# Two narrow projections with high and low weights side by side, and operands moved to multiples of 512 bytes

## The chip, the cores and the metric

The kernel runs on one core of a Trainium2 chip. The metric is the time of one execution on the device in microseconds (us), as the median of several runs. The engines are TensorE (PE; its weight loads are PEld), VectorE (DVE), ScalarE (ACT), GpSimd (POOL) and SyncE (SP), which here only issues loads. Each works through a queue of its own in order, and they wait for each other by semaphores.

## The reference, cut to what matters

A trunk of two layers over 256 tokens of width 2048, all in 32-bit floats. Layer 0 mixes with stick-breaking attention and gated linear attention, layer 1 with a Mamba-2 state-space mixer. Each layer ends in a squared-ReLU MLP and a gated embedding per layer.

```python
for i in range(2):
    hn = rms_norm(h, norm_mix[i])
    h = h + (sb_gla_mixer(hn, ...) if i == 0 else ssd_mixer(hn, ...))
    h = h + square(relu(rms_norm(h, norm_mlp[i]) @ w_up)) @ w_down
    h = h + sigmoid(h @ ple_w_gate[i]) * (p[i] @ ple_w_proj[i])
return rms_norm(h, final_norm)
```

Each mixer begins with one wide product of `hn` whose columns are then split. Two of the pieces are narrow. In layer 0 it is the gate rank: `glr`, 16 columns wide, goes through `sigmoid` and sums into the decays of the linear attention. In layer 1 it is `dt`, 64 columns: `dt = softplus(hn @ w + dt_bias)`, and the running sum of `dt * a` over each chunk of 128 tokens gives the decays of all 64 heads.

## The kernel before

**The products.** Every long product is made from reduced-precision pieces. A weight is split into a high part `whi` (a cast on ScalarE, L90) and the rest `wlo` (a subtract on VectorE, L91), and so is `x`; an `x` page holds for one slice of 128 features the 256 high values of all tokens and then the 256 low ones, 512 columns. In `feature_major` (L119 to L145) 128 weight columns are stationary and `x` moves: `whi` against all 512 columns (L130) gives hi·hi in the left half of a bank of PSUM and hi·lo in the right half, `wlo` against the 256 high columns (L135) adds lo·hi to the right half. `add_halves` (L167 to L173) puts the two together: ScalarE copies the right half out (L170), VectorE adds it to the left (L171) and in mixer 1 multiplies by the norm's factor (L173). `token_major` (L159 to L161) and the down product of the MLP (L344 to L346) have the weights as the moving operand of 512 columns, three products for a piece.

**The blocks.** Weights come in blocks of 128 x 2048 floats (1 MB, `load_block`, L102) through three buffers `wraw` on SyncE's queue. Each block is split in two halves of 1024 into three pairs of buffers `whi` and `wlo`. The MLP has a second set of such buffers in a pool of its own, and uses both in turn. A group of 512 weight columns takes four blocks, which is eight halves of 8 + 8 products.

**The narrow projections.** `ab_glr` (mixer 0) and `ssd_dt` (mixer 1, where the first x group follows) use `feature_major` with `width=1, kts=16`: the 16 or 64 columns are padded on the host to 128, so each is one block of 1 MB, two casts, two splits, 16 products of 512 columns and 16 of 256.

**After ssd_dt.** `dt_steps` computes softplus as a series on VectorE, some twenty small instructions on 64 x 256 values (L610 to L626; L614 is a reciprocal, L620 the series, L626 the running sum), which interleave with the convolution (L648), the gating (L179) and the scaling of `x` by the gain (L112, its input `hn` from GpSimd). The running sum goes out to memory (`acs_rows`, L627) and comes back broadcast over all partitions (`rb`, L659), both issued from ScalarE's queue; TensorE transposes `dt` and the sums (L631, L632). The first user of `rb` is L675 on VectorE (tile `mt`).

**What sets the order.** The code is a set of Python generators that are advanced in turn; the framework's scheduler then fixes the order of each engine's queue when the kernel is built. So an edit can move instructions far from its own line.

**Addresses.** Tiles are placed one behind the other in each pool. The profile and the built order show no addresses; from the tile sizes, the pages of `x` and the buffers of the pool `wts` (wraw, whi, wlo) begin at multiples of 512 bytes. The pool of the MLP (its whi, wlo and wsum) and four constants of mixer 0 begin 64 bytes past one, `h` 128 bytes and `ident` 384.

## Time and profile before

| | |
|---|---|
| runs | 2745.70, 2743.98, 2745.56 us; median 2745.56 |
| the profiled execution | 2747.21 us, of which its span on the core 2745.5 |
| granted clock of TensorE, mean | 0.996 |
| TensorE busy | 2711.9 us (14036 products); weight loads 2282.7 |
| VectorE, ScalarE, GpSimd busy | 1914.1, 1421.1, 167.5 us |
| loads | 511.69 MB, 186 GB/s on average |

In a timeline, a row gives the start and the busy time of one or several like instructions in us, then engine, line, operation, output and inputs with shapes and count; a bracket is idle time of the engine ahead of it and what ended it. Successive instructions overlap at their ends, so that the time from one start to the next is the price of an instruction, a little under its busy time. A line number is that of the kernel before; the same code stands 2 lines lower in the changed kernel up to L143, and 27 lines lower from there.

### The profile page before, as it was taken

How to read it: one execution, taken by the hardware profiler on the slowest of the kernel's cores; microseconds unless marked ns; L12 is line 12 of the kernel's file. 1: busy time of each engine (PE TensorE's matmuls, PEld its weight loads, DVE VectorE, ACT ScalarE, POOL GpSimd, SP SyncE). 2: the span in 40 equal slices, each digit the busy share in tenths (PEclk: the TensorE clock that was granted, in tenths of full speed). 3: DMA queues.
4: the chain of work that ended last, by engine and by line, in shares of the span. 5: the costliest groups of instructions: out<-in, count | busy, mean ns of one | idle time of the engine just before them, and what ended most of it. 6: DMA issues, size and time to landing. Idle time of an engine off the chain costs nothing.

```text
span 2745.5 us, 35718 instructions
## 1 busy us (share of the span) xinstructions
PE 2711.9 (99%) x14036; PEld 2282.7 (83%) x14036; DVE 1914.1 (70%) x2569; ACT 1421.1 (52%) x1933; POOL 167.5 (6%) x258
## 2 busy tenths in 40 slices
PE   8999999999999999999999999999999999999998
PEld 6888878888888888888888888888888888888886
DVE  7455666676867767558987878754677776776755
ACT  6455455545545445556555655644454544535544
POOL 2000000000000000002132122300000000000000
PEclk9999999999999999999999999999999999999999
DMA  6544355555555555454555555455555555555543
GB/s 246 186 167 153 123 184 184 199 187 195 201 184 198 186 191 206 176 185 157 197 197 180 192 190 179 170 188 194 184 200 186 209 188 184 186 197 187 214 178 146
DMA packets 73305, 511.69 MB, mean 186 GB/s; under 512 B 8672, under 2 KB 8864, under 8 KB 12464
## 3 DMA queue, kind: packets, MB, share of 16 engines
q1 hardware_dynamic: 70640, 498.63, 50.9%
q10 hardware_dynamic: 2496, 10.78, 1.1%
q8 instruction: 110, 1.80, 0.3%
q14 instruction: 59, 0.48, 0.0%
HBM read 507.21 MB, written 2.16 MB: 186 GB/s over the span
## 4 chain that ended last, share of the span: by engine, by line
PE 96%; DVE 2%; ACT 1%; issue 0%; DMA 0%; POOL 0%; DVEq 0%; ACTq 0%
PE acc L130 31%; PE acc L135 16%; PE q L344 8%; PE q L346 8%; PE q L345 8%; PE acct L160 6%; PE acct L159 6%; PE acct L161 6%; DVE wlo L91 1%; PE y_ps L718 1%; PE x_tp L253 1%; PE y_ps L720 0%; DVE x L112 0%; DVE a_cv L648 0%; ACT whi L90 0%
## 5 line engine op out<-in xcount | busy, mean ns | idle before, releaser
L91 DVE TENSOR_TENSOR wlo<-wraw,whi 128x1024 fp32r<-128x1024 f32 (+1 forms) x940 | 1137.6, 1217 | 657.7 <-ACT whi L90 653.5
L90 ACT CAST whi<-wraw 128x1024 fp32r<-128x1024 f32 x940 | 969.8, 1038 | 1027.4 <-PE acc L130 488.8
L130 PE MATMUL acc<-x,whi 128*128 128x512 f32 x3872 | 1224.0, 399 | 9.9 <-ACT whi L90 9.9
L135 PEld LDWEIGHTS acc<-x,wlo 128*128 128x128 f32 x3872 | 725.0, 189 | 178.4 <-DVE wlo L91 10.0
L135 PE MATMUL acc<-x,wlo 128*128 128x256 f32 x3872 | 761.0, 279 | 7.3 <-DVE wlo L91 7.3
L130 PEld LDWEIGHTS acc<-x,whi 128*128 128x128 f32 x3872 | 596.6, 189 | 19.3 <-ACT whi L90 10.1
L344 PE MATMUL q<-whi,hid 128*128 128x512 f32 x884 | 350.0, 396 | 0.1
L346 PE MATMUL q<-whi,hid 128*128 128x512 f32 x884 | 347.3, 393 | 0.0
L345 PE MATMUL q<-wlo,hid 128*128 128x512 f32 x884 | 344.9, 390 | 0.0
L346 PEld LDWEIGHTS q<-whi,hid 128*128 128x128 f32 x884 | 165.9, 188 | 39.8
L345 PEld LDWEIGHTS q<-wlo,hid 128*128 128x128 f32 x884 | 166.1, 188 | 37.1
L344 PEld LDWEIGHTS q<-whi,hid 128*128 128x128 f32 x884 | 166.0, 188 | 35.4 <-ACT whi L90 0.5
L159 PE MATMUL acct<-whi,x 128*128 128x512 f32 x384 | 151.0, 393 | 0.0
L161 PE MATMUL acct<-whi,x 128*128 128x512 f32 x384 | 149.8, 390 | 0.0
L160 PE MATMUL acct<-wlo,x 128*128 128x512 f32 x384 | 149.7, 390 | 0.0
L90 ACT CAST whi<-wsum 128x1024 fp32r<-128x1024 f32 x56 | 58.9, 1051 | 80.5 <-PE q L346 53.4
L161 PE MATMUL acct<-whi,yx 128*128 128x512 f32 x256 | 100.3, 392 | 0.0
L160 PE MATMUL acct<-wlo,yx 128*128 128x512 f32 x256 | 100.2, 391 | 0.0
L159 PE MATMUL acct<-whi,yx 128*128 128x512 f32 x256 | 100.2, 391 | 0.0
L91 DVE TENSOR_TENSOR wlo<-wsum,whi 128x1024 fp32r<-128x1024 f32 x56 | 68.5, 1223 | 30.1 <-ACT whi L90 30.1
L170 ACT COPY right<-acc 128x256 f32<-128x256 f32 x198 | 72.2, 368 | 27.2 <-PE acc L135 27.1
L161 PEld LDWEIGHTS acct<-whi,x 128*128 128x128 f32 x384 | 72.1, 188 | 15.0
(283 smaller groups left out, 2357.1 us busy)
## 6 DMA issues: line engine op xcount, KB each, us to landing
wraw<-in_mlp_up_dram SPq DMA_DIRECT2D x128, 1024.0 KB, 4.8
wraw<-in_mlp_down_dram SPq DMA_DIRECT2D x128, 1024.0 KB, 4.8
wraw<-in_ssd_in_dram SPq DMA_DIRECT2D x80, 1024.0 KB, 4.8
wraw<-in_ab_in_dram SPq DMA_DIRECT2D x47, 1024.0 KB, 4.8
wraw<-in_ple_gate_dram SPq DMA_DIRECT2D x32, 1024.0 KB, 4.8
wraw<-in_ssd_out_dram SPq DMA_DIRECT2D x32, 1024.0 KB, 4.8
wraw<-in_ab_out_dram SPq DMA_DIRECT2D x16, 1024.0 KB, 4.8
rb<-acs_rows ACTq DMA_DIRECT2D x8, 1024.0 KB, 4.8
```

Of the source, the lines that this page charges most:

```text
L90: nc.scalar.copy(out=hi, in_=src_raw)
L91: nc.vector.tensor_tensor(out=lo, in0=src_raw, in1=hi.bitcast(F32), op=ALU.subtract)
L130: nc.tensor.matmul(banks[n], lhsT=hi[:, o : o + P], rhs=xt(k), start=(k == 0), stop=False, skip_group_check=True)
L135: nc.tensor.matmul(banks[n][:, T : 2 * T], lhsT=lo[:, o : o + P], rhs=xt(k)[:, 0:T], start=False, stop=(k == kb_n * kts - 1), skip_group_c ...
L159: nc.tensor.matmul(banks[n], lhsT=xh, rhs=wh, start=(k == 0), stop=False, skip_group_check=True)
L160: nc.tensor.matmul(banks[n], lhsT=xh, rhs=wl, start=False, stop=False, skip_group_check=True)
L161: nc.tensor.matmul(banks[n], lhsT=xl, rhs=wh, start=False, stop=(k == kb_n * kts - 1), skip_group_check=True)
L170: nc.scalar.copy(out=right[:rows], in_=bank[:rows, T : 2 * T])
L253: nc.tensor.transpose(tp[:, j * T + t * P : j * T + t * P + P], h[:, t, (k + j) * P : (k + j + 1) * P], ident)
L344: nc.tensor.matmul(banks[b], lhsT=ah, rhs=wh, start=b not in begun, stop=False, skip_group_check=True)
L345: nc.tensor.matmul(banks[b], lhsT=ah, rhs=wl, start=False, stop=False, skip_group_check=True)
L346: nc.tensor.matmul(banks[b], lhsT=al, rhs=wh, start=False, stop=end and last[b] == m, skip_group_check=True)
```

## The change

Two things are done. First, spare tiles are put in, and `ident` is moved up, so that the operands of the long products begin at multiples of 512 bytes: what moves are `h`, `ident`, the MLP's second whi and wlo, its wsum, and the constants of mixer 0. The pages and the buffers of `wts` stay on multiples as they were.

Second, `narrow_major` takes the place of `feature_major` for the two narrow projections. The weights come unpadded (32 columns for ab_glr, which has 16; 64 for ssd_dt), a load of 256 KB or 512 KB into a tile of its own. High and low part lie side by side in one tile, so that 64 or 128 stationary columns [high, low] meet the 512 moving columns of `x` in one product: 16 products of 512 in all. The bank then holds hi·hi and hi·lo in its upper rows and lo·hi and lo·lo in its lower ones; `add_parts` copies out and adds the first three.

```diff
-    ev.tile([P, 8], F32, tag="spare", name="spare")
+    ev.tile([P, 136], F32, tag="spare", name="spare", bufs=1)
...
+    keep.tile([P, 96], F32, name="spare0")
     h = keep.tile([P, 2, D], F32, name="h")
+    ident = keep.tile([P, P], F32, name="ident")
...
-    keep.tile([P, 8], F32, name="spare")
+    keep.tile([P, 40], F32, name="spare1")
...
+    def narrow_major(src, cn, xt, evac, pool):
+
+        raw = pool.tile([P, KT, cn], F32, name="nraw")
+        nc.sync.dma_start(raw, src)
+        both = pool.tile([P, KT, 2, cn], F32R, name="wboth")
+        nc.scalar.copy(out=both[:, :, 0, :], in_=raw)
+        nc.vector.tensor_tensor(out=both[:, :, 1, :], in0=raw, in1=both[:, :, 0, :].bitcast(F32), op=ALU.subtract)
+        bank = acc_ps.tile([P, 512], F32, tag="acc", name="accn")
+        for k in range(KT):
+            nc.tensor.matmul(bank[: 2 * cn], lhsT=both[:, k, :, :].rearrange("p a c -> p (a c)"), rhs=xt(k),
+                             start=(k == 0), stop=(k == KT - 1), skip_group_check=True)
+        yield
+        evac(bank)
+        yield
+
+    def add_parts(dst, bank, cn, scale=None):
+        right = ev.tile([P, T], F32, tag="right", name="right")
+        low = ev.tile([P, T], F32, tag="right", name="low")
+        nc.scalar.copy(out=right[:cn], in_=bank[:cn, T : 2 * T])
+        nc.scalar.copy(out=low[:cn], in_=bank[cn : 2 * cn, 0:T])
+        nc.vector.tensor_tensor(out=dst, in0=bank[:cn, 0:T], in1=right[:cn], op=ALU.add)
+        nc.vector.tensor_tensor(out=dst, in0=dst, in1=low[:cn], op=ALU.add)
+        if scale is not None:
+            nc.vector.tensor_tensor(out=dst, in0=dst, in1=scale, op=ALU.mult)
...
-                add_halves(u, bank, 64, rstd[:64])
+                add_parts(u, bank, 64, rstd[:64])
...
-                        yield from feature_major([[ssd_dt]], 1, xu, evac_dt, width=1, kts=16)
+                        yield from narrow_major(ssd_dt, 64, xu, evac_dt, mid)
...
-                add_halves(glr, bank)
+                add_parts(glr[:32], bank, 32)
...
-                yield from feature_major([[ab_glr]], 1, x, evac_glr, width=1, kts=16)
+                yield from narrow_major(ab_glr, 32, x, evac_glr, mid)
```

The load, the cast (L152) and the subtract (L153) of the narrow weights have buffers of their own, so the scheduler puts them where it has room: for ab_glr among the first blocks of mixer 0, for ssd_dt into the first gate of the embedding of layer 0, between two of its loads (SyncE), casts and splits. In mixer 1 some hundred rows of VectorE and fifty of ScalarE around ssd_dt change places; nearly everything else keeps its order. ScalarE's issue of `rb` (L686 there) stood ahead of the cast of the fourth half of the next group, and now stands behind it (the cast of `whi_10892`).

Three places on VectorE's queue follow. The first is the middle of the group after ssd_dt in mixer 1: `dt_work` holds the series, `a_cv` the convolution, `bc0` its gated result, and `wlo_...` are the splits for which TensorE waits. Before:

```order
L613 TENSOR_SCALAR dt_work_10557<-dt_work_10557 64x256
L179 SCALAR_TENSOR_TENSOR bc0_10217<-th_10571,a_cv_10566 128x256
L614 RECIPROCAL dt_work_10557<-dt_work_10557 64x256
L648 SCALAR_TENSOR_TENSOR a_cv_10634<-xp_10484,cw_9986,a_cv_10634 128x256
L615 TENSOR_TENSOR dt_work_10557<-dt_work_10557 64x256
L648 SCALAR_TENSOR_TENSOR a_cv_10634<-xp_10484,cw_9986,a_cv_10634 128x256
L616 TENSOR_TENSOR dt_work_10557<-dt_work_10557 64x256
L91 TENSOR_TENSOR wlo_10653<-wraw_10650,whi_10652 128x1024
L179 SCALAR_TENSOR_TENSOR bc0_10217<-th_10639,a_cv_10634 128x256
L618 TENSOR_SCALAR dt_work_10557<-dt_work_10557 64x256
L91 TENSOR_TENSOR wlo_10673<-wraw_10650,whi_10672 128x1024
L620 SCALAR_TENSOR_TENSOR dt_work_10557<-dt_work_10557 64x256
```

and in the changed kernel:

```order
L675 SCALAR_TENSOR_TENSOR a_cv_10599<-xp_10467,cw_9969,a_cv_10599 128x256
L93 TENSOR_TENSOR wlo_10638<-wraw_10615,whi_10637 128x1024
L206 SCALAR_TENSOR_TENSOR bc0_10200<-th_10536,a_cv_10531 128x256
L640 TENSOR_SCALAR dt_work_10519<-dt_work_10519 64x256
L675 SCALAR_TENSOR_TENSOR a_cv_10599<-xp_10467,cw_9969,a_cv_10599 128x256
L641 RECIPROCAL dt_work_10519<-dt_work_10519 64x256
L675 SCALAR_TENSOR_TENSOR a_cv_10599<-xp_10467,cw_9969,a_cv_10599 128x256
L642 TENSOR_TENSOR dt_work_10519<-dt_work_10519 64x256
L114 SCALAR_TENSOR_TENSOR x2_9981<-hn_10657,gain_83,x2_9981 128x256
L643 TENSOR_TENSOR dt_work_10519<-dt_work_10519 64x256
L206 SCALAR_TENSOR_TENSOR bc0_10200<-th_10604,a_cv_10599 128x256
L645 TENSOR_SCALAR dt_work_10519<-dt_work_10519 64x256
```

The first split here stands behind the reciprocal (L614) before, and ahead of it (now L641) after. It is also that of a later half of its group: before, `wlo_10653` is the third of the eight halves; after, `wlo_10638` is the fourth.

The second place is some 60 rows on, at the seventh and eighth half of the next group; `xs` is the gated convolution of the x group and `mt` the decay matrix. Before:

```order
L680 TENSOR_TENSOR mt_10959<-mt_10959,cb_10901 128x1024
L648 SCALAR_TENSOR_TENSOR a_cv_11012<-xp_10820,cw_9986,a_cv_11012 128x256
L675 TENSOR_SCALAR mt_10959<-rb_10896,acs_t_10001 128x128
L648 SCALAR_TENSOR_TENSOR a_cv_11012<-xp_10820,cw_9986,a_cv_11012 128x256
L675 TENSOR_SCALAR mt_10959<-rb_10896,acs_t_10001 128x128
L648 SCALAR_TENSOR_TENSOR a_cv_11012<-xp_10820,cw_9986,a_cv_11012 128x256
L675 TENSOR_SCALAR mt_10959<-rb_10896,acs_t_10001 128x128 x6
L91 TENSOR_TENSOR wlo_11033<-wraw_11030,whi_11032 128x1024
```

and in the changed kernel:

```order
L707 TENSOR_TENSOR mt_10924<-mt_10924,cb_10866 128x1024
L93 TENSOR_TENSOR wlo_10958<-wraw_10935,whi_10957 128x1024
L675 SCALAR_TENSOR_TENSOR a_cv_10977<-xp_10785,cw_9969,a_cv_10977 128x256
L702 TENSOR_SCALAR mt_10924<-rb_10861,acs_t_9984 128x128
L675 SCALAR_TENSOR_TENSOR a_cv_10977<-xp_10785,cw_9969,a_cv_10977 128x256
L702 TENSOR_SCALAR mt_10924<-rb_10861,acs_t_9984 128x128
L675 SCALAR_TENSOR_TENSOR a_cv_10977<-xp_10785,cw_9969,a_cv_10977 128x256
L702 TENSOR_SCALAR mt_10924<-rb_10861,acs_t_9984 128x128 x6
L206 SCALAR_TENSOR_TENSOR xs_10766<-th_10982,a_cv_10977 128x256
L93 TENSOR_TENSOR wlo_10998<-wraw_10995,whi_10997 128x1024
```

One gating instruction (L206, before L179) now stands ahead of the seventh half's split instead of behind it, and the product `mt` by `cb` (L707, before L680) has moved in between the two splits ahead.

The third place is in mixer 0, the end of the first group; `x3` are pages of `x`. Before:

```order
L112 SCALAR_TENSOR_TENSOR x3_132<-hn_628,gain_77,x3_132 128x256
L112 SCALAR_TENSOR_TENSOR x3_132<-hn_632,gain_77,x3_132 128x256
L112 SCALAR_TENSOR_TENSOR x3_132<-hn_636,gain_77,x3_132 128x256
L91 TENSOR_TENSOR wlo_565<-wraw_542,whi_564 128x1024
L112 SCALAR_TENSOR_TENSOR x3_132<-hn_640,gain_77,x3_132 128x256
L91 TENSOR_TENSOR wlo_655<-wraw_652,whi_654 128x1024
```

and in the changed kernel:

```order
L114 SCALAR_TENSOR_TENSOR x3_133<-hn_629,gain_83,x3_133 128x256
L114 SCALAR_TENSOR_TENSOR x3_133<-hn_633,gain_83,x3_133 128x256
L114 SCALAR_TENSOR_TENSOR x3_133<-hn_637,gain_83,x3_133 128x256
L153 TENSOR_TENSOR wboth_1322<-nraw_1320,wboth_1322 128x16x32
L93 TENSOR_TENSOR wlo_566<-wraw_543,whi_565 128x1024
L114 SCALAR_TENSOR_TENSOR x3_133<-hn_641,gain_83,x3_133 128x256
L93 TENSOR_TENSOR wlo_656<-wraw_653,whi_655 128x1024
```

The new subtract L153 stands between the scaling of three pages and the split of the last half.

More of the change, by code (lines that the diff above doesn't have):

```diff
@@ L65, in small_ps @@
         return sm_ps.tile([P, cols], F32, tag="sm", name=name, padded_shape=[P, 512])
+    keep.tile([P, 96], F32, name="spare0")
     h = keep.tile([P, 2, D], F32, name="h")
+    ident = keep.tile([P, P], F32, name="ident")
+    make_identity(nc, ident)
     gain = keep.tile([P, 4, KT], F32, name="gain")
     nc.scalar.dma_start(gain, gains)
-    ident = keep.tile([P, P], F32, name="ident")
-    make_identity(nc, ident)
     ones = keep.tile([P, P], F32, name="ones")
@@ L597, in mixer1, with evac_dt @@
             acs_rows = dram.tile([64, T], F32, name="acs_rows")
-            def evac_dt(n, bank):
+            def evac_dt(bank):
                 work = page([P, 8, T], "dt_work")[:64]
                 u = work[:, 0, :]
-                add_halves(u, bank, 64, rstd[:64])
+                add_parts(u, bank, 64, rstd[:64])
                 sides.append([None, 1, dt_steps(work)])
@@ L926, in mixer0, with evac_glr @@
             gsum = mid.tile([P, 4, T], F32, name="gsum")
-            def evac_glr(n, bank):
-                add_halves(glr, bank)
+            def evac_glr(bank):
+                add_parts(glr[:32], bank, 32)
             def sb_all():
@@ L1092, in blocks, with narrow @@
         return c(w.reshape(k // (kts * 128), kts, 128, n // 512, 512).transpose(3, 0, 2, 1, 4)).reshape(-1, 128, kts * 512)
-    def narrow(w):
+    def narrow(w, cn):
         k, n = w.shape
-        w = np.pad(w, ((0, 0), (0, 128 - n)))
-        return c(w.reshape(k // 128, 128, 128).transpose(1, 0, 2)).reshape(128, -1)
+        w = np.pad(w, ((0, 0), (0, cn - n)))
+        return c(w.reshape(k // 128, 128, cn).transpose(1, 0, 2))
     def cols(v):
@@ L1115, in layout @@
         "ab_in": blocks(np.concatenate([ab[:, :5120], ab[:, 5136:]], axis=1)),
-        "ab_glr": narrow(ab[:, 5120:5136]),
+        "ab_glr": narrow(ab[:, 5120:5136], 32),
         "gate_up": c(a["ab_w_gate_up"][0].reshape(16, 4, 128)),
@@ L1121, in layout @@
         "ssd_in": blocks(ssd_cols),
-        "ssd_dt": narrow(sw[:, 10240:]),
+        "ssd_dt": narrow(sw[:, 10240:], 64),
         "conv": c(np.concatenate([a["ssd_conv_w"][0], a["ssd_conv_b"][0][None]], axis=0).reshape(5, 48, 128).transpose(2, 1, 0)),
```

## The prediction

> **What bounds the kernel now.** I read the page first: how busy each engine is, and which engine owns the chain of work that ended last.
>
> ```profile
> PE 2711.9 (99%) x14036; PEld 2282.7 (83%) x14036; DVE 1914.1 (70%) x2569; ACT 1421.1 (52%) x1933; POOL 167.5 (6%) x258
> ...
> PE 96%; DVE 2%; ACT 1%; issue 0%; DMA 0%; POOL 0%; DVEq 0%; ACTq 0%
> ```
>
> TensorE is busy for 2711.9 of 2745.5 us and owns 96% of the chain. So only three things can move the time: fewer TensorE instructions, or less of the 33.6 us in which it idles, or less time at a low granted clock. Second I asked for busy time by stretches around the two places that the diff touches, which gave this table (PE, PEld, DVE, ACT, POOL busy; then the granted clock).
>
> ```profile
> core 0: us, PE busy (x) PEld busy (x) DVE busy (x) ACT busy (x) POOL busy (x), PEclk, DMA share, GB/s
> 29.16:32.57 3.41, 1.19 (x8) 0.80 (x7) 1.39 (x7) 3.37 (x5) 0.00 (x0) 1.00 0.08 31
> 32.57:35.99 3.41, 3.41 (x12) 2.82 (x12) 3.41 (x3) 1.88 (x3) 2.40 (x2) 0.50 0.09 19
> 1281.97:1287.54 5.57, 5.57 (x35) 4.91 (x34) 5.57 (x14) 4.49 (x7) 0.03 (x1) 1.00 0.72 269
> 1287.54:1298.92 11.38, 7.57 (x42) 6.18 (x40) 11.34 (x23) 7.31 (x15) 3.97 (x7) 1.00 0.25 92
> 1298.92:1305.74 6.82, 5.28 (x18) 4.71 (x19) 6.82 (x12) 2.48 (x4) 3.14 (x3) 0.50 0.38 127
> 1305.74:1318.80 13.06, 13.06 (x75) 11.00 (x74) 11.49 (x22) 5.33 (x7) 0.80 (x1) 1.00 0.54 181
> 1318.80:1342.80 24.00, 24.00 (x144) 20.77 (x142) 23.67 (x53) 18.09 (x31) 3.03 (x7) 1.00 0.66 244
> ```
>
> The four rows from 1287.54 on are the first full group of four blocks after the ssd_dt projection, and the start of the next. VectorE is busy in all of 1281.97 to 1305.74 (5.57 of 5.57, 11.34 of 11.38, 6.82 of 6.82), and TensorE is not: 7.57 of 11.38, then 5.28 of 6.82, and those at a clock of 0.50. So here the bound is VectorE. Third, the timeline of TensorE in that stretch:
>
> ```profile
> 1287.54 0.63 PE L130 MATMUL acc<-x,whi 128*128 128x512 f32 x2
> ...
> 1300.46 2.07 PE L135 MATMUL acc<-x,wlo 128*128 128x256 f32 x8 [5.35 <-DVE wlo L91]
> ...
> 1318.80 0.63 PE L130 MATMUL acc<-x,whi 128*128 128x512 f32 x2
> ```
>
> The row at 1300.46 shows the stall: 5.35 us until VectorE had split a block (wlo, L91). The group of 16 by 4 products runs from 1287.54 to 1318.80, 31.26 us. Its work is eight halves of 8 products of 512 columns and 8 of 256. The ssd_dt projection is two such halves, and took 5.57 us (the row 1281.97:1287.54 of the table). So eight take 22.28 us, and 8.98 us of the group are lost. Fourth, VectorE in the same stretch, with the idle time before an instruction in brackets:
>
> ```profile
> 1288.64 1.21 DVE L91 TENSOR_TENSOR wlo<-wraw,whi 128x1024 fp32r<-128x1024 f32 x1
> 1289.77 0.41 DVE L179 SCALAR_TENSOR_TENSOR bc<-th,a_cv 128x256 f32<-128x256 f32 x1
> ...
> 1290.50 0.41 DVE L171 TENSOR_TENSOR dt_work<-acc,right 64x256 f32<-64x256 f32 x1
> 1290.84 0.47 DVE L648 SCALAR_TENSOR_TENSOR a_cv<-xp,cw,a_cv 128x256 f32<-128x256 f32 x1
> ...
> 1299.19 1.21 DVE L91 TENSOR_TENSOR wlo<-wraw,whi 128x1024 fp32r<-128x1024 f32 x1
> ...
> 1310.59 1.23 DVE L91 TENSOR_TENSOR wlo<-wraw,whi 128x1024 fp32r<-128x1024 f32 x1 [0.75 <-ACT whi L90]
> ...
> 1316.59 0.29 DVE L633 COPY dt_t<-dt_tp 128x128 f32<-128x128 f32 x1 [0.82 <-PE dt_tp L632]
> ...
> 1320.17 0.42 DVE L171 TENSOR_TENSOR xp<-acc,right 128x256 f32<-128x256 f32 x1 [0.29 <-ACT right L170]
> ...
> 1328.24 0.28 DVE L675 TENSOR_SCALAR mt<-rb,acs_t 128x128 f32<-128x128 f32 x1
> ...
> 1337.11 1.21 DVE L91 TENSOR_TENSOR wlo<-wraw,whi 128x1024 fp32r<-128x1024 f32 x1
> ```
>
> Between 1288 and 1328 only three gaps have a bracket (0.75, 0.82, 0.29 us): a wait for a cast, for a transpose on TensorE, and for a copy out of TensorE's bank. The last row matters because TensorE used that block at once:
>
> ```profile
> 1338.37 1.22 PE L135 MATMUL acc<-x,wlo 128*128 128x256 f32 x8
> ```
>
> The split that began at 1337.11 ends at 1338.32; TensorE takes it up at 1338.37. So up to here VectorE sets TensorE's pace, and what VectorE saves before 1337.11 is what TensorE can gain.
>
> **The change, part by part.**
>
> *A, the gate-rank projection (ab_glr).* TensorE's timeline there:
>
> ```profile
> 152.55 1.98 PE L130 MATMUL acc<-x,whi 128*128 128x512 f32 x8
> 154.37 1.11 PE L135 MATMUL acc<-x,wlo 128*128 128x256 f32 x8
> 155.32 2.00 PE L130 MATMUL acc<-x,whi 128*128 128x512 f32 x8
> ...
> 158.11 0.60 PE L543 MATMUL z<-q,k__644 128*128 128x256 f32 x2
> ```
>
> Eight products of 512 columns take 154.37 − 152.55 = 1.82 us, 0.228 each, eight of 256 take 0.95 us (155.32 − 154.37). The sixteen products of 256 columns go; the sixteen of 512 stay, now with 64 stationary columns. No row has a product of 512 moving columns with 64 stationary ones; the nearest is the 128 wide one at 0.228, and I take that. The other bound is that it costs what the pair of products costs now, 0.346: then nothing is gained (R4). TensorE is gapless there. −1.90 us, all on the path. Two casts and two splits go too, and one copy and one add of 32 rows come; off the path here.
>
> *B, the inserted split in mixer 0.* The new L152 and L153 stand early, while TensorE still waits on VectorE:
>
> ```profile
> 59.04 1.75 DVE L112 SCALAR_TENSOR_TENSOR x<-hn,gain,x 128x256 fp32r<-128x256 f32 x3
> 60.72 1.21 DVE L91 TENSOR_TENSOR wlo<-wraw,whi 128x1024 fp32r<-128x1024 f32 x1
> ```
>
> ```profile
> 62.08 0.41 PE L135 MATMUL acc<-x,wlo 128*128 128x256 f32 x2
> ```
>
> The split at 60.72 ends at 61.93, and TensorE starts on it at 62.08: no slack. The new subtract (128 x 512 elements) now stands just ahead of it, and behind it wait that split and so TensorE. A 1024-element split holds VectorE 1.13 us (1288.64 to 1289.77), half of that is 0.57. Bounds: 0 (more work ahead in an in-order queue cannot bring the split sooner, so no gain), and 1.21, a whole split. I take +0.57 by the row of its own kind. The load of 256 KB replaces one of 1 MB on SyncE's queue and goes out ahead of the sixth weight block; ScalarE's extra cast fits in its idle time there.
>
> *C, mixer 1 (ssd_dt).* Up to the split at 1337.11 VectorE does two L91 fewer (2 x 1.13) and one add of 64 x 256 more (0.34, 1290.50 to 1290.84): −1.92. The changed order puts one more L206 (in before L179, 0.34 likewise an add of that size) ahead of the same block: −1.58. The three gaps sum to 1.86; with TensorE earlier I expect them all but gone, −1.7. Sum −3.3 us, and TensorE takes it over since it was waiting there.
>
> Could TensorE itself be the limit? Without VectorE its group begins 1.90 us earlier, at 1285.64. In the new order the first three halves are split beforehand, so it runs to 1285.64 + 3 x 2.785 = 1294.0, and 0.46 us on needs the block wlo_10638. That split loses four things ahead of it: what stood from 1295.63 on (the 3.56 us from L613 to the split at 1299.19, now behind it) and one L91; it gains one add: 1299.19 − 3.56 − 1.13 + 0.34 = 1294.84, done at 1296.0, a wait of 1.5 us. The second wait, for wlo_10670, comes out at 2.9 us in the same manner. The group would end some 6 us earlier than 1318.80, and then run into VectorE's bound. So VectorE's −3.3 decides; −6.5 is the bound if it did not, −1.9 the bound if VectorE's gaps come back elsewhere and the second split's relief only fills them.
>
> Does the wait of 2.9 us bring back the half clock? In the first stretch of the table TensorE was busy 1.19 of 3.41 us, idle 2.22, and the clock granted over the next 3.41 us was 0.50. By that row the wait may cost half of 3.41 us, 1.7. It would lie in the stretch that VectorE bounds, as the half clock of 1298.92 to 1305.74 does now, so the sum has nothing for it; R2 has it in full. [...]
>
> The last link is the broadcast rb, loaded from acs_rows, which VectorE's first L702 (in before L675, 1328.24) needs:
>
> ```profile
> rb<-acs_rows ACTq DMA_DIRECT2D x8, 1024.0 KB, 4.8
> ```
>
> ```profile
> 1318.81 1.05 ACT L90 CAST whi<-wraw 128x1024 fp32r<-128x1024 f32 x1
> 1319.58 0.34 ACTq L659 DMA_DIRECT2D rb<-acs_rows  x1
> ```
>
> Before, the load was issued at 1319.58, landed 4.8 us later (1324.4), and was needed at 1328.24: 3.8 us to spare. After, ScalarE's queue holds the issue behind a cast (whi_10892) that needs the first half of the next group. With that group beginning 6 or 3.3 us earlier than 1318.80, the half (2.79) and the cast (1.05, L90 above) put the issue at 1316.6 or 1319.3 and the landing at 1321.4 or 1324.1; VectorE comes to its L702 at 1328.24 − 3.3 = 1324.9. Some 1 to 3 us are left: no cost.
>
> *D, the addresses.* The pages and the three weight buffers began at multiples of 512 bytes before and still do; what moves there are the second pair of whi and wlo (by the mlp pool), its wsum, h, ident and the small constants, from 64, 128 or 384 bytes past one. The down products of the mlp use both pairs in turn as the moving operand, so the trace holds the comparison: a half on the aligned pair, on the other, and on the aligned one again.
>
> ```profile
> 1116.41 0.40 PE L344 MATMUL q<-whi,hid 128*128 128x512 f32 x1
> ...
> 1119.18 0.40 PE L344 MATMUL q<-whi,hid 128*128 128x512 f32 x1
> ...
> 1121.95 0.40 PE L344 MATMUL q<-whi,hid 128*128 128x512 f32 x1
> ```
>
> 2.77 us from the first row to the second, 2.77 from the second to the third. So 0; over the some 480 triples (three products each) that use the second pair a difference of 2.5 ns in 693 would be 1.2 us: bounds ±1.2.
>
> *E, the inserted split in the first ple group.* The ssd_dt weights are now loaded and split a whole stage early, between two gates.
>
> ```profile
> L102 SPq DMA_DIRECT2D wraw<-in_ple_gate_dram x3: 328/328/328, 1121.7 to 1135.1; - x3
> ```
>
> ```profile
> 1145.04 0.37 ACT L108 CAST x<-x_tp 128x256 fp32r<-128x256 f32 x1 [1.35 <-DVE x L109]
> ```
>
> ```profile
> 1147.82 0.39 PE L161 MATMUL acct<-whi,x 128*128 128x512 f32 x1
> ```
>
> Its load waits on SyncE's queue for the end of the mlp at 1133, ahead of the gate load of 1135.1 (the last of the three): nothing is held up. The cast (1.05) and the subtract (1.13) fall where ScalarE idled 1.35 us, and the gate's products need their block only when those running until 1147.82 are through. Cover: those queued products. If it failed, 1.2 us.
>
> Sum: A −1.90, B +0.57, C −3.3, D 0, E 0: −4.6 us. The profiled execution took 2747.21 us and would become 2742.6; it lies 1.65 above the median of the runs, 2745.56, from which I count: 2740.9. A measurement of this kernel can tell about 0.2% from no change, which is 5.5 us (below 2740.1 or above 2751.1).
>
> **The rivals.**
>
> *R1, TensorE keeps more.* If VectorE does its rows faster in the new order than in the old, the walk of C along TensorE holds: mixer 1 gives 5.7 to 6.5 us, −7 to −7.6 in all, 2738. For it: the stall of 5.35 us is the largest there is. Against it: VectorE's 23.67 of 24.00 us from 1318.80 on. 22%.
>
> *R2, the relief is given back.* The three gaps stay (C keeps −1.58) and the half clock of the new wait falls on products that VectorE no longer covers (+1.7): with A and B −1.2, 2744.3. For it: the idle stretch at 29 us and the clock behind it. Against it: the gaps hang on TensorE, which comes earlier. 20%.
>
> *R3, slower.* VectorE reaches its first L702 before rb is there. Its queue is in order, so the splits wlo_10938 and wlo_10958 stand behind and TensorE stops. From a landing of 5.8 us (4.8 and the 1 to spare) each us costs one; at 10.4 the gain is gone; at 14 us it is 2745.56 − 4.6 + 8.2 + 1.7 (clock) = 2750.9, slower than before. For it: the issue now stands behind a cast that waits for TensorE. Against it: eight such loads with a median of 4.8. 5%.
>
> *R4, the addresses matter after all,* somewhere the rows above don't show, or the change does nothing because the narrow products cost as much as before: −7 or so, or −0.5. 4%.
>
> **How the numbers follow.** The forecast has 49%, by itself from 2739.5 to 2742.3 (C from its bound −1.9 to −4.7, as far on the other side). Faster by over 0.2% (under 2740.1): R1 nearly whole, 0.21, the lower third of the forecast, 0.15, and 0.02 of R4: 0.38. Slower (over 2751.1): the far end of R3 and what I have not thought of, 0.05. Within: 0.57. The range takes R1's bound (−7.6 with D's −1.2: 2736.8) and R2 with B at 1.21 and D at +1.2 (2746.1), rounded outward: 2736.5 to 2746.5. Outside lie R3, half of R4 and the corners where several bounds meet.
>
> **What would show it.** Right: ab_glr at 3.65 us instead of 5.56; the stall of 5.35 us replaced by two of 1 to 3 us; no gap before VectorE's first L702; the halves on the second pair still at 2.77 us; the block at 62.08 about 0.6 later. Wrong: a product of 512 columns with 64 or 128 stationary columns [hi, lo] dearer than 0.228 us; halves at another price all over, which would be the addresses; an idle VectorE ahead of L702 (R3); or a next group in mixer 1 that starts over 5 us earlier and stays so (R1).

## The result, and the profile after

The changed kernel takes 2729.18 us (median of 4 runs, 2728.90 to 2729.53) against 2745.27 before (4 runs, 2743.98 to 2745.70): a ratio of 0.9942 with a 95% interval of 0.9926 to 0.9957. It is 16.1 us faster, where 4.6 were forecast, and below the range. The profiled execution took 2729.36 us, with a span of 2727.6 and a mean granted clock of 0.997 (before 2747.21, 2745.5, 0.996). The page of after begins with

```profile
PE 2694.5 (99%) x14004; PEld 2275.1 (83%) x14004; DVE 1908.3 (70%) x2569; ACT 1418.4 (52%) x1933; POOL 174.3 (6%) x258
```

TensorE has lost 17.4 us of busy time with 32 products fewer. At 0.119 us each (0.95 for eight, in part A of the prediction) those account for 3.8. About 2 more are near what the half clock of 1298.92 to 1305.74 added before and not in the change (an estimate: half of 5.28 us of busy time at a clock of 0.50, 2.6). The rest is products that have become cheaper. To see where, I took the same product of TensorE in both traces and subtracted its two start times. The offset of after against before, at before's time:

| stretch | offset goes | gain | what lies there |
|---|---|---|---|
| 0 to 50 | 0 to −1.1 | 1.1 | start, half clock granted in another stretch (from 31.01 us, before from 32.57) |
| 50 to 100 | −1.1 to −0.5 | −0.6 | term B |
| 100 to 175 | −0.5 to −2.4 | 1.9 | term A |
| 500 to 1150 | −2.4 to −8.1 | 5.8 | first MLP |
| 1150 to 1270 | −8.1 to −8.15 | 0 | term E |
| 1270 to 1400 | −8.15 to −11.7 | 3.55 | term C |
| 1950 to 2725 | −11.8 to −17.8 | 6.0 | second MLP |

The 1.1 us at the start are put down to no edit: two kernels that each have one part of the change show 2.5 and 1.0 there. The two MLPs give 11.8 us, and the offset moves only in their down products (at 610, 800 and 990 it is −3.9, −5.4 and −6.9, one step for each quarter). The groups of the page say the same. Of before, the down product's three lines and, for comparison, the same form in the token-major stages:

```profile
L344 PE MATMUL q<-whi,hid 128*128 128x512 f32 x884 | 350.0, 396 | 0.1
L346 PE MATMUL q<-whi,hid 128*128 128x512 f32 x884 | 347.3, 393 | 0.0
L345 PE MATMUL q<-wlo,hid 128*128 128x512 f32 x884 | 344.9, 390 | 0.0
...
L159 PE MATMUL acct<-whi,x 128*128 128x512 f32 x384 | 151.0, 393 | 0.0
L161 PE MATMUL acct<-whi,x 128*128 128x512 f32 x384 | 149.8, 390 | 0.0
L160 PE MATMUL acct<-wlo,x 128*128 128x512 f32 x384 | 149.7, 390 | 0.0
```

and of after, the down products and the token-major lines:

```profile
L371 PE MATMUL q<-whi,hid 128*128 128x512 f32 x884 | 344.7, 390 | 0.0
L373 PE MATMUL q<-whi,hid 128*128 128x512 f32 x884 | 344.0, 389 | 0.0
L372 PE MATMUL q<-wlo,hid 128*128 128x512 f32 x884 | 344.0, 389 | 0.0
...
L186 PE MATMUL acct<-whi,x 128*128 128x512 f32 x384 | 151.1, 393 | 0.0
L188 PE MATMUL acct<-whi,x 128*128 128x512 f32 x384 | 149.7, 390 | 0.0
L187 PE MATMUL acct<-wlo,x 128*128 128x512 f32 x384 | 149.7, 390 | 0.0
```

The down lines fell from 396, 393 and 390 ns to 390, 389 and 389; the token-major lines stayed. Successive products overlap (389 or 390 ns of busy time each in the change, 227 from start to start), so the price is the time from start to start. The three halves that the prediction showed at 2.77 us each read, on TensorE's timeline of after,

```profile
1108.60 0.39 PE L371 MATMUL q<-whi,hid 128*128 128x512 f32 x1
...
1111.32 0.39 PE L371 MATMUL q<-whi,hid 128*128 128x512 f32 x1
...
1114.04 0.39 PE L371 MATMUL q<-whi,hid 128*128 128x512 f32 x1
```

12 products in 2.72 us, the half on the first buffers and the half on the second alike. Over the whole trace I use the mean time of a triple (the three products L344 to L346, start to start): before, 693.9 ns in halves on the first buffers and 691.5 on the second; after, 682.1 and 680.0. That is 11.7 ns on each of 996 triples, 11.6 us.

The narrow products, from the timeline of TensorE in mixer 0 of after:

```profile
152.03 3.83 PE L156 MATMUL accn<-x,wboth 128*64 128x512 f32 x16
155.70 0.59 PE L570 MATMUL z<-q,k__645 128*128 128x256 f32 x2
```

3.67 us from start to start, where 5.56 stood. And the block ahead of it that had no slack:

```profile
61.47 0.50 PE L137 MATMUL acc<-x,wlo 128*128 128x256 f32 x2 [0.35 <-DVE wlo L93]
```

It now waits 0.35 us for VectorE; it had no bracket. In mixer 1, the waits of TensorE after the dt projection:

```profile
1273.82 3.80 PE L156 MATMUL accn<-x,wboth 128*128 128x512 f32 x16
...
1287.28 0.50 PE L137 MATMUL acc<-x,wlo 128*128 128x256 f32 x2 [0.85 <-DVE wlo L93]
...
1293.45 1.22 PE L137 MATMUL acc<-x,wlo 128*128 128x256 f32 x8 [1.75 <-DVE wlo L93]
...
1300.94 0.50 PE L137 MATMUL acc<-x,wlo 128*128 128x256 f32 x2 [0.22 <-DVE wlo L93]
...
1304.68 0.27 PE L658 MATMUL dt_tp<-ident,dt_work 64*128 64x64 f32 x1 [1.96 <-DVE dt_work L651]
...
1327.32 1.21 PE L137 MATMUL acc<-x,wlo 128*128 128x256 f32 x8
```

The one stall of 5.35 us has become four of 4.78 in sum. VectorE of after, at the places where the prediction spoke of gaps and of `rb`, and at the end of the stretch:

```profile
1299.66 1.22 DVE L93 TENSOR_TENSOR wlo<-wraw,whi 128x1024 fp32r<-128x1024 f32 x1 [1.23 <-ACT whi L92]
...
1316.12 0.86 DVE L702 TENSOR_SCALAR mt<-rb,acs_t 128x128 f32<-128x128 f32 x4
...
1326.06 2.34 DVE L93 TENSOR_TENSOR wlo<-wraw,whi 128x1024 fp32r<-128x1024 f32 x2
```

The first L702 stands without a bracket. The first of the two splits at 1326.06 ends at about 1327.2, and TensorE is on the block at 1327.32: VectorE sets the pace there as before.

### The profile page after: what moved, and what is told of

Its sections match the earlier page's. It is cut to its first block, busy times and chain, and to the rows that moved or that the text cites. A ratio compares the mean times of both kernels' runs of the same rounds, so it can differ in the third digit from the quotient of the medians.

```text
span 2727.6 us, 35652 instructions
## 1 busy us (share of the span) xinstructions
PE 2694.5 (99%) x14004; PEld 2275.1 (83%) x14004; DVE 1908.3 (70%) x2569; ACT 1418.4 (52%) x1933; POOL 174.3 (6%) x258
## 4 chain that ended last, share of the span: by engine, by line
PE 95%; DVE 3%; ACT 1%; issue 1%; POOL 0%; DMA 0%; DVEq 0%; ACTq 0%
PE acc L132 31%; PE acc L137 15%; PE q L371 8%; PE q L373 8%; PE q L372 8%; PE acct L187 7%; PE acct L186 7%; PE acct L188 7%; DVE wlo L93 1%; PE y_ps L745 1%; PE x_tp L280 1%; PE y_ps L747 0%; DVE x L114 0%; DVE a_cv L675 0%; ACT whi L92 0%
## 5 line engine op out<-in xcount | busy, mean ns | idle before, releaser
L92 ACT CAST whi<-wraw 128x1024 fp32r<-128x1024 f32 (+1 forms) x936 | 964.7, 1038 | 1007.5 <-PE acc L132 478.1
L137 PEld LDWEIGHTS acc<-x,wlo 128*128 128x128 f32 x3840 | 716.9, 188 | 175.7 <-DVE wlo L93 9.2
L137 PE MATMUL acc<-x,wlo 128*128 128x256 f32 x3840 | 753.4, 279 | 5.2 <-DVE wlo L93 5.1
L371 PE MATMUL q<-whi,hid 128*128 128x512 f32 x884 | 344.7, 390 | 0.0
L373 PE MATMUL q<-whi,hid 128*128 128x512 f32 x884 | 344.0, 389 | 0.0
```

What stands on the lines that cost most here:

```text
L92: nc.scalar.copy(out=hi, in_=src_raw)
L137: nc.tensor.matmul(banks[n][:, T : 2 * T], lhsT=lo[:, o : o + P], rhs=xt(k)[:, 0:T], start=False, stop=(k == kb_n * kts - 1), skip_group_c ...
L371: nc.tensor.matmul(banks[b], lhsT=ah, rhs=wh, start=b not in begun, stop=False, skip_group_check=True)
L373: nc.tensor.matmul(banks[b], lhsT=al, rhs=wh, start=False, stop=end and last[b] == m, skip_group_check=True)
```

## The experiments

Two questions were open: which address made the down products cheaper and by what rule, and whether the narrow part behaves as its working said. "Before there" is the kernel before on the same chip. A time with (1) is a single run, so that differences of a few us between such times are read from the triples and the offsets. The first letters in the expectations: P, that moving the MLP's second buffers does it, against N, that the narrow projections do; then S and M, that what counts is whether the operands share a remainder or mismatch, against A, that they must begin at multiples themselves; then R, reads by TensorE, against W, writes of other engines into the buffers. Other letters are explained where they stand. A "remainder" is below always that of a start address by 256 bytes.

| kernel | median us (runs) | before there | first / second buffers, ns a triple |
|---|---|---|---|
| before | 2745.27 (4) | | 693.9 / 691.5 |
| the change | 2729.18 (4) | 2745.27 | 682.1 / 680.0 |
| pool_only | 2733.68 (5) | 2746.19 | 684.0 / 680.2 |
| narrow_only | 2742.34 (11) | 2746.19 | 693.5 / 691.4 |
| after_pool64 | 2741.11 (10) | 2746.19 | 693.3 / 691.4 |
| after_wts64 | 2742.94 (10) | 2746.19 | 687.8 / 700.0 |
| all64 | 2733.10 (4) | 2745.51 | 682.2 / 680.0 |
| pool32 | 2745.78 (1) | 2745.47 | 690.4 / 700.8 |
| pool128 | 2740.55 (1) | 2745.51 | 686.6 / 697.7 |
| pool256 | 2729.17 (1) | 2745.51 | 682.2 / 680.0 |
| whi64 | 2746.19 (1) | 2745.51 | 691.1 / 698.4 |
| wlo64 | 2741.15 (1) | 2746.02 | 689.5 / 693.7 |
| wsum64 | 2729.67 (1) | 2745.47 | 682.1 / 680.0 |
| wts256 | 2730.06 (1) | 2746.02 | 682.2 / 680.0 |
| wts_gap64 | 2736.54 (1) | 2745.47 | 688.2 / 686.7 |
| vector_extra | 2732.71 (1) | 2746.02 | 682.2 / 680.0 |
| glr_through_wraw | 2729.70 (4) | 2746.02 | 682.2 / 680.0 |

**The two parts apart.** *pool_only* is the kernel before with one spare tile made larger:

```diff
-    ev.tile([P, 8], F32, tag="spare", name="spare")
+    ev.tile([P, 136], F32, tag="spare", name="spare", bufs=1)
```

> The kernel before with one spare tile made larger, so that the MLP's second whi, wlo and wsum begin at a multiple of 512 bytes; h, ident, and both narrow projections stay as before, and so do the addresses of the pages and of the first buffers. Theory P (the second buffers' 64 bytes cost the down products some 3.8 ns each, 2988 of them): 11 to 11.6 us faster than before, triples of the down product at 681 ns instead of 693, in the halves on the first buffers too. Rival N (h, ident or the shift of everything by 512 bytes does it): within 1 us of before.

A ratio of 0.9957 (0.9945 to 0.9970), 12.5 us faster. The first line of the down products and TensorE's stall in mixer 1, from its page and its timeline:

```profile
L344 PE MATMUL q<-whi,hid 128*128 128x512 f32 x884 | 344.9, 390 | 0.7 <-DVE h L441 0.7
```

```profile
1291.79 2.07 PE L135 MATMUL acc<-x,wlo 128*128 128x256 f32 x8 [4.84 <-DVE wlo L91]
```

The down products are as cheap as in the change while the old stall stands: P holds, N falls.

*narrow_only* is the changed kernel with the spare tiles and the place of `ident` of before:

```diff
-    ev.tile([P, 136], F32, tag="spare", name="spare", bufs=1)
+    ev.tile([P, 8], F32, tag="spare", name="spare")
...
-    keep.tile([P, 40], F32, name="spare1")
+    keep.tile([P, 8], F32, name="spare")
```

> The narrow projections of the changed kernel with the addresses of the kernel before. Theory P: the terms A, B and C of the prediction alone, -1.9 + 0.6 - 3.6 = -4.9 us (between 4 and 6 us faster), the down products' triples still at 693 ns. Rival N: the same if the addresses of h and ident do nothing here; but if the narrow projections in some way quicken the down products, 16 us faster.

A ratio of 0.9988 (0.9979 to 0.9996): 3.85 us, a little under what the narrow part was given. Its 11 runs lie between 2740.20 and 2744.94, and the profiled one is the slowest. In it the offset against before goes from −0.4 to −2.3 at ab_glr and from −2.26 to −1.95 over mixer 1, so there C gave nothing in that run. The windows show why: between 1310 and 1320 it has clocks of 0.95 and 0.71.

```profile
1310.00:1315.00 5.00, 3.03 (x16) 2.03 (x16) 4.91 (x11) 2.00 (x4) 0.51 (x1) 0.95 0.50 192
1315.00:1320.00 5.00, 5.00 (x20) 4.27 (x21) 5.00 (x13) 2.87 (x6) 0.61 (x2) 0.71 0.23 43
```

Its triples are those of before. The two parts add up, 12.5 and 3.85 to 16.35 where the change gave 16.1; with a spread of 4.7 us in narrow_only, so close a match is partly chance.

**Which address.** Three kernels differ from the changed one by the sizes of spare tiles alone. *after_pool64* puts the MLP's second buffers back to 64 bytes past a multiple (`[P, 152]` for `[P, 136]`):

> The changed kernel with the spare tile 64 bytes larger: the MLP's second whi, wlo and wsum lie 64 bytes past a multiple of 512 again, all else stays on multiples. Theory P: 11 us slower than the changed kernel, about 5 us faster than before, triples at 693 ns. Rival N: as fast as the changed kernel, 16 us faster than before.

It is 11.9 us slower than the change, with the triples of before; its down lines are those of before too:

```profile
L371 PE MATMUL q<-whi,hid 128*128 128x512 f32 x884 | 350.1, 396 | 0.0
```

*after_wts64* does the reverse: the pages (with the stationary `hid`) and the first buffers go 64 bytes past, and the second buffers stay on multiples.

```diff
-    ev.tile([P, 136], F32, tag="spare", name="spare", bufs=1)
+    ev.tile([P, 120], F32, tag="spare", name="spare", bufs=1)
...
-    keep.tile([P, 40], F32, name="spare1")
+    keep.tile([P, 56], F32, name="spare1")
```

> The changed kernel with the pages of x and hid and the first three wraw, whi and wlo 64 bytes past a multiple of 512, and the MLP's second buffers on multiples. Theory P, as far as the trace goes (a moving weight operand 64 past costs 5, -1, 2 ns in a triple, and casts into such a buffer some more): token-major triples from 681 to 687 ns and down triples near 693, in all 11 to 20 us slower than the changed kernel; feature-major products, whose moving operand is now 64 past too, may add 3872 times 2 to 4 ns. If only the pair of unlike addresses in one stage matters (rival M), the token-major products keep 681 and only the down products slow down.

The down products are slow again, now more in the halves on the aligned second buffers (700.0), while the token-major and feature-major stages, whose operands all lie 64 past, keep their price: the median triple there is 680 ns, the feature-major pair 233 and 115 (before 680, 233 and 116).

```profile
L186 PE MATMUL acct<-whi,x 128*128 128x512 f32 x384 | 151.1, 393 | 0.0
```

So a common remainder of 64 costs no more there than one of 0. *all64* tests just that: only the second edit (`[P, 56]`), so that pages, first and second buffers all lie 64 past.

> The changed kernel with all long operands 64 bytes past a multiple of 512: pages, both sets of whi, wlo, and wraw, wsum alike. Theory S (what costs is that operands of one stage differ in their remainder; a common remainder is free): as fast as the changed kernel, 16 to 17 us faster than before, down triples at 681 ns. Rival A (each operand has to begin at a multiple of 512): down triples at 693 ns or more, 11 to 13 us slower than the changed kernel.

The triples are 682.2 and 680.0, the best there are, with no operand on a multiple: S holds, A falls. The whole is 4 us slower than the change (2733.10; ratio 0.9955, 0.9938 to 0.9972), and all of that comes in mixer 1, where its offset against after goes from −1.2 at 1270 to +3.1 at 1345. Its windows there, and then those of the change:

```profile
1300.00:1305.00 5.00, 2.79 (x13) 2.18 (x13) 5.00 (x12) 1.68 (x4) 0.79 (x1) 0.90 0.64 210
1305.00:1310.00 5.00, 5.00 (x17) 3.75 (x17) 3.56 (x11) 3.13 (x6) 0.00 (x0) 0.50 0.06 16
1310.00:1315.00 5.00, 5.00 (x29) 4.44 (x29) 5.00 (x8) 1.51 (x3) 2.15 (x2) 0.92 0.53 170
```

```profile
1300.00:1305.00 5.00, 2.83 (x16) 1.88 (x15) 5.00 (x10) 2.27 (x4) 0.78 (x1) 1.00 0.61 210
1305.00:1310.00 5.00, 5.00 (x28) 4.08 (x29) 5.00 (x14) 4.04 (x7) 0.00 (x0) 1.00 0.06 16
```

With the same wait of about 2 us (1.97 here at L658, 1.96 in the change) one got the half clock and the other did not.

**The period.** *pool32*, *pool128* and *pool256* put only the second buffers 32, 128 and 256 bytes past a multiple of 512 (`[P, 144]`, `[P, 168]`, `[P, 200]`).

> The changed kernel with the MLP's second buffers 32 bytes past. If only the remainder by 256 counts, and any but 0 costs, as 64 and 128 do: triples at 687 to 693 ns, 8 to 12 us slower than the changed kernel. If reads come in pieces of 64 bytes: 681 ns, or worse than with 64, since every piece straddles two.

> The changed kernel with the MLP's second buffers 128 bytes past a multiple of 512, all else on one. Theory S with a period of 512 bytes: down triples at 687 to 693 ns as with 64. If the period is 128 or less: 681 ns.

> The changed kernel with the MLP's second buffers 256 bytes past a multiple of 512, all else on one. With a period of 512 bytes: down triples above 685 ns. If the period is 256 (the one product of the narrow projections that had its stationary operand 256 past ran at 227 ns, as fast as any): 681 ns, as fast as the changed kernel.

256 costs nothing (682.2 and 680.0 ns a triple), 128 and 32 do (686.6 and 697.7, 690.4 and 700.8), 32 not less than 64 (693.3 and 691.4 in after_pool64). So of the offsets tried the remainder by 256 counts, not by 512, and the cost does not grow in step with the distance.

**Which buffer, and who is disturbed.** In the changed kernel, pads inside the second set move one buffer of it at a time by 64 bytes; *whi64* moves `whi`, *wlo64* `wlo`, *wsum64* the MLP's wsum, which TensorE does not read in these products.

```diff
+        if second:
+            pool.tile([P, 16], F32, tag="pad0", name="pad0", bufs=1)
         hi = pool.tile([P, cols], F32R, tag="whi", name="whi", padded_shape=[P, 1024])
+        if second:
+            pool.tile([P, 112], F32, tag="pad1", name="pad1", bufs=1)
         lo = pool.tile([P, cols], F32R, tag="wlo", name="wlo", padded_shape=[P, 1024])
```

> The changed kernel with only the MLP's second whi 64 bytes past; second wlo and wsum stay on multiples. If TensorE pays as it reads a moving operand whose remainder differs: in halves on the second buffers the first and third product of a triple slow down (232 and 229 ns), the second (wlo) stays at 227, and the halves on the first buffers stay at 681 a triple. If it is the write of a cast or a split that disturbs it: the halves on the first buffers, during which ScalarE writes the second whi, slow down as well.

> The changed kernel with only the MLP's second wlo 64 bytes past a multiple of 512; second whi and wsum stay on multiples. Theory R (TensorE pays for reads whose remainders differ, also between one product and the next): in the halves on the second buffers the triples rise from 681 to 690 ns or so, as with the second whi alone. Theory W (the writes by the cast and the split disturb it): the halves on the first buffers slow down while VectorE writes the second wlo, later in the half than before (second to fourth triple), and the first triple stays at 681.

> The changed kernel with only wsum 64 bytes past: no product reads it, only VectorE and ScalarE do. Theory R: as the changed kernel, all triples at 681 ns, 16 us faster than before. Theory W (other engines' accesses at unlike remainders disturb TensorE): triples dearer in the MLP's seven-product blocks.

Either of the two operands is enough, `whi` (two products of three read it; 691.1 and 698.4 ns a triple) more than `wlo` (689.5 and 693.7); wsum does nothing (682.1 and 680.0). In whi64 the halves on the untouched first buffers slowed as well, which its expectation had put down to writes. wlo64 decides it. There the first triple on the second buffers takes 227, 237 and 241 ns (medians): the cost begins with the first product that reads the moved `wlo`. In whi64 it is 237, 241 and 231, dear from the first product, which reads `whi`. The first buffers are then disturbed from their first product on and recover towards the end of the half, and a write does not fit that:

```profile
1113.68 0.40 PE L380 MATMUL q<-whi,hid 128*128 128x512 f32 x1
...
1115.76 0.39 PE L380 MATMUL q<-whi,hid 128*128 128x512 f32 x1
...
1116.44 0.39 PE L380 MATMUL q<-whi,hid 128*128 128x512 f32 x1
```

```profile
1115.02 1.23 DVE L102 TENSOR_TENSOR wlo<-wraw,whi 128x1024 fp32r<-128x1024 f32 x1 [1.60 <-ACT whi L101]
```

The first three triples of this half average 693 ns, and the last, under VectorE's split, takes 680. So W falls: the cost goes with what TensorE itself reads and has just read. The same recovery can be read in the kernel before. The medians of its three products, in ns, by the triple's place in the half:

| | 1st triple | 2nd | 3rd | 4th |
|---|---|---|---|---|
| first buffers | 234, 231, 233 | 236, 224, 231 | 236, 228, 232 | 231, 227, 227 |
| second buffers | 236, 235, 231 | 232, 226, 229 | 232, 226, 229 | 232, 226, 229 |

On the first buffers both operands lie on multiples, and yet the second and third triple are dearer there; the cost has nearly gone by the fourth. On the second buffers the remainders differ, and it settles at 232, 226, 229.

**Unlike everywhere, without a switch.** A gap tile at the head of the pool `wts` moves all buffers of weights, first and second, by 256 bytes (*wts256*) or by 64 (*wts_gap64*), while the pages stay on multiples.

```diff
+    wts.tile([P, 64], F32, tag="gap", name="gap", bufs=1)
```

> The changed kernel with all weight buffers 256 bytes past a multiple of 512 and the pages on one. If the period of the effect is 256 bytes, for every pair of stationary and moving operand: as fast as the changed kernel within 1 us, 16 us faster than before. If it holds for the down products alone: token-major or feature-major products change their price (227, 233 and 116 ns now) and the time moves by several us either way.

> The changed kernel with all weight buffers, first and second set and wsum, 64 bytes past a multiple of 512 and the pages on multiples, so that moving and stationary operand differ in every long product. Theory R: down triples at 690 ns and more without recovery in any half, token-major triples up from 681 to 690 to 700 (2400 products, 7 to 15 us), and feature-major products dearer too, if it is the same reading: in all 20 to 50 us slower than the changed kernel. Rival D (it is something of the down products or of the MLP's pool alone): token-major at 227 and feature-major at 233 and 116 ns as now, and no more than 12 to 17 us slower.

256 is free here too (682.2 and 680.0). At 64 I expected a loss of tens of us, since now every product has unlike operands, and that was a miss: it is some 7 us slower than the change, of which 1.0 lies at the start and 1.1 in mixer 1, where it had the half clock. The page's down and token-major lines:

```profile
L374 PE MATMUL q<-whi,hid 128*128 128x512 f32 x884 | 348.1, 394 | 0.0
L373 PE MATMUL q<-wlo,hid 128*128 128x512 f32 x884 | 346.2, 392 | 0.0
L372 PE MATMUL q<-whi,hid 128*128 128x512 f32 x884 | 344.4, 390 | 0.0
...
L187 PE MATMUL acct<-whi,x 128*128 128x512 f32 x384 | 151.7, 395 | 0.0
L188 PE MATMUL acct<-wlo,x 128*128 128x512 f32 x384 | 150.8, 393 | 0.0
L189 PE MATMUL acct<-whi,x 128*128 128x512 f32 x384 | 150.1, 391 | 0.0
```

Unlike operands cost 6 to 7 ns a triple of the down product in every place of a half, and 7 ns in the median token-major triple (687 for 680). Kernels whose buffers switch between remainders pay 10 to 14 on the mean of both halves (wlo64 10.5, before 11.7, pool32 14.4). Not all of that is the switch: how dear an unlike half stays depends on which remainders meet. The fourth triple on the second buffers takes 687 ns in before, 696 in wlo64, 700 in after_wts64 and 702 in pool32 (medians), and no run shows why. Products became dearer when the addresses of their two operands were unlike (693.9 and 691.5 ns a triple in before, 682.1 and 680.0 in the change). Whether the two reads hinder each other, or what else does it, the runs do not show.

**Mixer 1 and mixer 0.** *vector_extra* adds six instructions to VectorE behind the dt projection of the changed kernel, work that nothing uses:

```diff
                 add_parts(u, bank, 64, rstd[:64])
+                for _ in range(6):
+                    nc.vector.tensor_tensor(out=work[:, 7, :], in0=u, in1=rstd[:64], op=ALU.mult)
```

> The changed kernel with six products of 64 x 256 more on VectorE after the ssd_dt evacuation (their result isn't used), about 2.0 us of its time. If VectorE sets the pace of mixer 1 to the place at 1337 us, as part C has it: the gain there shrinks by 1.5 to 2 us, the whole is 14 to 14.6 us faster than before. Rival R1 (TensorE alone): no difference to the changed kernel in mixer 1.

Against the change it loses 4.1 us over mixer 1 (offset from −1.0 at 1270 to +3.1 at 1345) where 1.5 to 2 were expected, and that is twice the 2.0 us of the six instructions. The edit changed the order too, as the timeline of TensorE shows:

```profile
1288.62 1.21 PE L137 MATMUL acc<-x,wlo 128*128 128x256 f32 x8 [1.85 <-DVE wlo L93]
1296.91 2.08 PE L137 MATMUL acc<-x,wlo 128*128 128x256 f32 x8 [5.24 <-DVE wlo L93]
```

The stall is back, with the half clock behind it (0.50 between 1295 and 1300). So TensorE waits for VectorE in this stretch and does not set the pace alone. Whether the added work or the new order cost the 4.1 us, and the price per us of VectorE, the run does not show.

*glr_through_wraw* loads the raw gate-rank weights into a `wraw` buffer, which puts them in the turn of the blocks and so keeps the cast and subtract away from the early split:

```diff
-        raw = pool.tile([P, KT, cn], F32, name="nraw")
+        if cn == 32:
+            raw = wts.tile([P, KT, cn], F32, tag="wraw", name="nraw", padded_shape=[P, KT, 128])
+        else:
+            raw = pool.tile([P, KT, cn], F32, name="nraw")
```

> The changed kernel with the gate-rank weights loaded into a buffer wraw, in turn with the other blocks, so that their split can't be put among the first blocks of mixer 0. Part B then goes: 0.5 to 0.6 us faster than the changed kernel (16.6 us faster than before), no wait of TensorE for a later split around 60 us. Rival: the wait is there in any case, and the time is the changed kernel's.

The wait is gone,

```profile
61.39 0.42 PE L137 MATMUL acc<-x,wlo 128*128 128x256 f32 x2
```

and 0.6 us between 50 and 100 with it, but the start (0.45) and mixer 1 (0.8) came out later by more: 2729.70 (4 runs; ratio 0.9939, 0.9922 to 0.9955), which cannot be told from the change's 2729.18. No version was measurably faster than the change.

## Why the prediction was wrong, step by step

**A, −1.90: right.** Sixteen products of 512 columns with 64 stationary ones took 3.67 us (3.65 forecast); the offset moved by −1.9.

**B, +0.57: right.** The block came 0.6 us later against its surroundings. By glr_through_wraw the split's place is the cause, since it went with the wait.

**C, −3.3: near in its total, −3.55, and partly by luck.** VectorE still hands TensorE its block without slack at the end of the stretch (1326.06 and 1327.32). The split that the forecast named began at 1326.06 instead of 1337.11, 11.05 us earlier. Of these 8.15 had been gained before the stretch, so C gave 2.9 there; the last 0.65 came behind that split. The term of the gaps was too large: they fell by 0.6 (1.86 to 1.23) where 1.7 were forecast, and a gap of 1.23 us appeared where none had been. VectorE's rows gave the other 2.3, where 1.58 were forecast. The walk along TensorE was wrong in detail too. The wait for wlo_10638 was 0.85 (1.5 forecast) and the one for the next split 1.75 (2.9 forecast), and two came that it did not have: 0.22 for a split, and the longest, 1.96, for the transpose of `dt_work` (L658).

**R1 and R3 did not come.** Mixer 1 gave 3.55, not R1's 5.7 to 6.5. In R3's place `rb` was issued at 1309.11 on ScalarE's queue and needed at 1316.12:

```profile
1309.11 0.34 ACTq L686 DMA_DIRECT2D rb<-acs_rows  x1
```

The list of DMA issues, for this load alone, has

```profile
rb<-acs_rows ACTq DMA_DIRECT2D x1, 1024.0 KB, 5.0
```

so it landed at 1314.1 and left 2.0 us to spare, within the 1 to 3 of the forecast. The prediction's 4.8 was the median of eight loads; the first load of before took 6.6, and had 2.1 us to spare instead of 3.8. **R2** did not come in the change's profile, but its half clock is real. Of the 15 profiles with the new narrow projections 11 have it in this stretch (not the change, pool256, wsum64 and glr_through_wraw). Mixer 1 then took from nothing (wts256) to 4.3 us (all64) longer than in the change, where R2 had 1.7. So the −3.55 of C is what it gives without the half clock; in narrow_only's profile C gave nothing.

**E, 0: right.** The offset does not move between 1150 and 1270.

**D, 0 with bounds of ±1.2: wrong, and with it the forecast.** It measured −11.6 by the triples, −12.5 by pool_only (1.5 us of it at the start). The prediction's opening already left it out: of what can move the time it named fewer instructions, less idle time and less low clock, but not cheaper instructions. The step that failed is the comparison: a half on the aligned buffers against one on the other buffers, 2.77 us each, hence "So 0". It took for granted that a half on the aligned buffers is undisturbed. It is not: after a half with other remainders it costs as much for three of its four triples (698, 691 and 696 ns, against 702, 687 and 687 on the second buffers), so both sides of the comparison carried the cost. The control had to come from a stage that never touches the second buffers, and the prediction held one without using it: in A, eight products of the same width take 0.228 us each, and 2.77 us for 12 are 0.231. The down products had a control as well: the very first half of them in before, ahead of any use of the second buffers.

```profile
519.18 0.40 PE L344 MATMUL q<-whi,hid 128*128 128x512 f32 x1
...
521.91 0.40 PE L344 MATMUL q<-whi,hid 128*128 128x512 f32 x1
```

Its 12 products take 2.73 us, not 2.77. The difference of 3.3 ns over 2988 down products is 9.9 us, R4's "−7 or so" and more, which had 4% with the narrow products' failure. The page's lines had it too, 396, 393 and 390 against 393, 390 and 390.

## What to carry to other kernels

Give all operands that TensorE reads in long products the same remainder by 256 bytes, above all buffers that take turns. Here a common remainder of 0 or of 64 took 682 and 680 ns a triple (the change, all64) and buffers in turn at unlike ones 692 to 696 on the mean of both halves, and one spare tile in the pool was worth 12.5 us (pool_only). When a trace is to show that something costs nothing, take the control from a stage that the suspect cannot reach, since the neighbour in the same loop may carry the same cost. And where a kernel has thousands of like instructions, compare their price between stages to the nanosecond before costing any edit: 4 ns on 2988 products outweighed all that the narrow projections saved.

## What was unexpected of the hardware

- In a row of products of 512 moving columns, each cost 227 ns from start to start when moving and stationary operands began at the same remainder by 256 bytes, 229 when all weights lay 64 bytes past the pages (wts_gap64), and 230 to 232 on the mean when buffers in turn differed (wlo64, before, pool32). Offsets of 32, 64 and 128 bytes cost, 256 does not (696, 692, 692 and 681 ns a triple on the mean of both halves, in pool32, after_pool64, pool128 and pool256).
- The cost outlasts its cause by one to three triples, 0.7 to 2 us: in before the halves on the first buffers, whose operands both lie on multiples, take 698, 691 and 696 ns and then 685. The same is seen behind the alternating products of 512 and 256 columns: in the change, where all operands are alike, the first triple of down products takes 690 ns and the next ones 680. What in TensorE or in the memory holds that state, no run shows.
- In wts_gap64 the feature-major products behave otherwise: the medians rise from 233 and 116 ns to 235 and 118, while the mean of the wide one falls from 237.9 to 236.3. That is unexplained.
- A wait of 2.0 us on TensorE was followed by a clock of 0.50 in all64 and by none in the change. In every profile the clock changes at whole multiples of 3.413 us from its other changes: in before, 32.57 and 1298.92 lie 371 such steps apart. In all64 (first row) the wait lay almost wholly in one step, in the change (second row) its last 0.5 us fell into the next:

```profile
1300.58:1303.99 3.41, 1.48 (x9) 1.03 (x8) 3.41 (x7) 1.04 (x3) 0.79 (x1) 1.00 0.82 257
1300.77:1304.18 3.41, 1.78 (x9) 1.34 (x9) 3.41 (x7) 1.50 (x3) 0.78 (x1) 1.00 0.66 209
```

TensorE was busy for 43% of the one and 52% of the other. Of all such steps at full clock in the 17 profiles, from 20 to 2700 us, the 17 in which TensorE was busy for less than 48% were each followed by the half clock, of the 24 between 48 and 55% eight were, and none above. The wait of 1.97 us in all64 is the longest there between 1284 and 1322. The changes stand at other times in other profiles: the first one to 0.50 comes at 32.57 us in before, at 31.01 in the change and at 30.29 in pool32.
